# A plain first unit, swapped banks, tables in thirty pieces, and weight sums made by accumulating transfers

## The chip, the cores and the metric

The kernel runs on one core of a Trainium2 chip. The core has a matrix engine (TensorE, PE in the profile, with its weight loads as PEld), a vector engine (VectorE, DVE), a scalar engine (ScalarE, ACT), a general one (GpSimd, POOL) and an engine that issues transfers (SyncE, SP), each with its own instruction queue that runs in order. Sixteen DMA engines move data between the chip's memory (HBM) and the core's on-chip memory. The metric is the device time of one launch in microseconds (us), the median over runs. The profile is one further execution.

## The reference

A stack of two layers over 512 tokens of width 1024, in 32-bit floats. Each layer is a half-step feed-forward block, a mixing block and another half-step feed-forward block, each behind an RMS norm; a last norm ends it.

```python
def swiglu(h, w_gate, w_up, w_down):
    return (jax.nn.silu(h @ w_gate) * (h @ w_up)) @ w_down

for l in range(DEPTH):                                  # DEPTH = 2
    x = x + 0.5 * swiglu(rmsnorm(x, ffn1_norm[l]), ...)  # FFN1, D_FF = 2816
    h = rmsnorm(x, mix_norm[l])
    ...                                                  # pooling heads, dilated attention with rotary q, k
    x = x + mixed @ w_out[l]
    x = x + 0.5 * swiglu(rmsnorm(x, ffn2_norm[l]), ...)  # FFN2
return rmsnorm(x, final_norm)
```

## The kernel before

The activations are kept transposed: `x[c]` is a tile of 128 channels by 512 tokens, c from 0 to 7. Every product of 32-bit numbers is made of three matmuls: each operand is split into a high part, rounded by a copy on ScalarE (`whi`, L357; `ah`), and a rest, which VectorE subtracts (`wlo`, L360; `al`), and high by high, low by high and high by low are added up.

A feed-forward block walks over six *units* of the 2816 hidden columns (`UNITS`, L38): first a small unit of 256, then five big units of 512. The gate and up products of a unit are not done plainly: activations and weights are cut into two by two blocks (token halves and channel halves against channel halves and gate/up columns), and seven products of sums of blocks are formed instead of eight (`PORD`, L39, is their order; `norm.block` picks the activation side). The sums of activations (`s_n`, `sh_n`, `sl_n`) are made once a block by `norm.fold` (L421), the sums of weight quarters for each unit anew by VectorE: `total` (L251) adds three quarters in two steps (L254, L258) for product 6, `every` (L264) adds that sum to a fourth (L266) for product 4, `across` (L260) adds two (L262) for product 7. A big unit does this twice (`cp` 0 and 1), so eight such sums of 128x1024; a small unit has four. The seven results are put together in `evacuate` (L616) on their way out of the accumulator banks: `px_f` holds products 1, 6, 7 and 4, `pz_f` products 2, 5 and 3. There are two banks under each of the tags A and B, and units alternate which tag `px_f` gets (L609).

After a unit's products, its hidden activations are transposed (`pt_f`, L600) during the next unit, and its down products (`pd_f`, L382 to L384) are put between that unit's steps; their result is added to `x` (L708). A steady unit on PE is 168 matmuls of 512 columns for the gate and up products, 96 for the down products, and 16 transposes.

The weights come through a list of jobs in the order of their use. `take` (L367) hands out a job's split weights, splits the job that stands two further on (`AHEAD`), and then `pump` (L332) starts as many loads of 512 KB as the cap of eleven live tiles lets it, all on SP's queue. `later`, `lazy` and `slow` are lists of work for VectorE and ScalarE, emitted by `flush` (L198) one step on.

At a block's start `norm.square` (L472) and `finish_col` (L489) sum squares on PE (`ms_n`), and one small power on POOL (L498) gives the norm's factor. Results of the first unit wait for it before they can be scaled. In layer 0's FFN1 this runs in `startup` (L119), while `x` is still being loaded.

The rotary tables (cosine and sine of position times frequency) are made by a generator (`tables`, L149) whose pieces of five to seven VectorE operations are called at the end of steps 6 and later in units 1 and 2 of the very first FFN1 (L683).

Of the kernel before, what the change touches and what calls it, by code (L numbers as in the profile page):

```python
# [10 lines left out]
F32 = mybir.dt.float32  # L11
F32R = mybir.dt.float32r
# [4 lines left out]
P = 128  # L17
S = 512
# [60 lines left out]
def trunk(ctx: ExitStack, tc: tile.TileContext, a: dict):  # L79
# [39 lines left out]
    def startup(norm):  # L119
# [21 lines left out]
        for c in range(KD):  # L141
            norm.fold(c)
            if c < 2:
                divide(c)
            if c == 4:
                divide()
            flush()

    def tables():  # L149
# [26 lines left out]
        reduce(turn)  # L176
        yield
        add_times(turn, far, M2)
        add_times(turn, far, M3)
        reduce(turn)  # L180
        yield
        nc.vector.tensor_tensor(ang, ang, turn, op=ALU.add)
        reduce(ang)
# [6 lines left out]
        nc.vector.tensor_tensor(k, k, k, op=ALU.mult)  # L190
        nc.vector.tensor_scalar(cosT, k, -2.0, 1.0, op0=ALU.mult, op1=ALU.add)
# [12 lines left out]
    class Load:  # L204


        def __init__(self, src, n, temps=0):
            self.src, self.n, self.temps, self.tile = src, n, temps, None

    class Job:  # L210


        def __init__(self, key, n, needs, get, pre=None, done=None):
            self.key, self.n, self.needs, self.get, self.pre, self.done = key, n, needs, get, pre, done
            self.part = None
# [3 lines left out]
    state = {"live": 0, "temps": 0, "load": 0, "split": 0, "taken": 0, "cap": SLOTS}  # L219
# [9 lines left out]
    def product_jobs(i, l, u):  # L229
# [3 lines left out]
        made, out = {}, []  # L233
# [12 lines left out]
        first = next(iter(made.values()))  # L246
        first.temps = cps
        loads.extend(made.values())
        both = {}

        def total(cp):  # L251

            b11, b12, b22 = (made[q + (cp,)].tile for q in ((0, 0), (0, 1), (1, 1)))
            nc.vector.tensor_tensor(b11, b11, b12, op=ALU.add)  # L254
            both[cp] = t4([P, D], F32, f"sum_{i}{l}_{u}_{cp}")
            state["live"] += 1
            state["temps"] -= 1
            nc.vector.tensor_tensor(both[cp], b11, b22, op=ALU.add)  # L258

        def across(cp):  # L260
            b12, b22 = made[0, 1, cp].tile, made[1, 1, cp].tile
            nc.vector.tensor_tensor(b12, b12, b22, op=ALU.add)  # L262

        def every(cp):  # L264
            b21 = made[1, 0, cp].tile
            nc.vector.tensor_tensor(b21, b21, both[cp], op=ALU.add)  # L266
            free()

        for p in PORD:
            for cp in range(cps):  # L270
                q = {k: made[k + (cp,)] for k in quarters + [(0, 1), (1, 1)]}
# [822 lines left out]
```

## Time and profile before

| what | value |
|---|---|
| median of 3 runs | 1922.75 us (1921.74 to 1922.85) |
| the profiled execution's own time | 1919.58 us |
| its span, first to last instruction | 1917.8 us |
| mean granted clock of PE | 0.986 of full |
| PE busy | 1857.2 us, 97% |
| VectorE busy | 1444.4 us, 75% |
| ScalarE busy | 950.4 us, 50% |
| POOL busy | 116.9 us, 6% |

PE is the engine that is nearly always busy. The span is read by looking where it is not, and at which clock it runs. Busy shares of the other engines are means over stages with different limits, so each stage has to be looked at by itself.

### The profile page before, as it was taken

The page shows a single profiled execution, that of the slowest core. Times are in us where ns is not written, and L with a number is a line of the kernel's source. Part 1 is how long each engine was busy: PE and PEld are TensorE (multiplying, and loading weights), DVE is VectorE, ACT ScalarE, POOL GpSimd, SP SyncE. Part 2 cuts the span into 40 slices and gives each one's busy share as a digit, 9 for nine tenths or more (in the row PEclk, how much of TensorE's full clock was granted, in tenths as well). Part 3 has the DMA queues.
Part 4 walks back from the last instruction along what each step waited for, and adds up shares of the span by engine and source line. Part 5 has one row for each costly group of instructions (what it writes and reads, how often), then busy time and mean ns, then how long its engine had stood idle before and what let it go on. Part 6 is the DMA issues. An engine that isn't in the chain of part 4 may idle for free.

```text
span 1917.8 us, 23563 instructions
## 1 busy us (share of the span) xinstructions
PE 1857.2 (97%) x8966; PEld 1551.3 (81%) x8966; DVE 1444.4 (75%) x2041; ACT 950.4 (50%) x1474; POOL 116.9 (6%) x105
## 2 busy tenths in 40 slices
PE   6989999999999999999989999999999989999998
PEld 5868888898877888888878888888888778888887
DVE  6996677647887986778688777675688688777675
ACT  6444344436665553444464444444476565444444
POOL 0000000013230000000000000000323200000000
PEclk7999999999999999999999999999999999999999
DMA  5223333125451233422313322340454223232321
GB/s 183 88 79 100 128 110 107 64 76 145 113 158 56 66 121 99 132 96 97 105 50 116 121 88 88 99 148 17 126 134 126 89 94 116 99 99 96 102 77 45
DMA packets 59696, 194.36 MB, mean 101 GB/s; under 512 B 7920, under 2 KB 8064, under 8 KB 59584
## 3 DMA queue, kind: packets, MB, share of 16 engines
q1 hardware_dynamic: 59440, 192.57, 31.9%
q8 instruction: 70, 1.15, 0.2%
q0 software_dynamic: 144, 0.29, 0.1%
q14 instruction: 42, 0.34, 0.1%
HBM read 171.87 MB, written 2.10 MB: 91 GB/s over the span
## 4 chain that ended last, share of the span: by engine, by line
PE 86%; DVE 8%; ACT 2%; issue 2%; DMA 1%; POOL 1%; SPq 0%; DVEq 0%; POOLq 0%; ACTq 0%
PE pd_f L384 8%; PE pd_f L383 8%; PE pd_f L382 8%; PE px_f L658 8%; PE px_f L655 8%; PE px_f L657 8%; PE pz_f L655 6%; PE pz_f L658 6%; PE pz_f L657 6%; PE pv_m L747 3%; PE ps_m L814 2%; PE pt_m L827 2%; PE pt_f L600 2%; DVE wlo L360 1%; PE po_m L843 1%
## 5 line engine op out<-in xcount | busy, mean ns | idle before, releaser
L360 DVE TENSOR_TENSOR wlo<-raw,whi 128x1024 fp32r<-128x1024 f32 (+2 forms) x421 | 502.0, 1198 | 55.4 <-ACT whi L357 50.4
L357 ACT ACTIVATE whi<-raw 128x1024 fp32r<-128x1024 f32 (+2 forms) x421 | 421.7, 1026 | 220.3 <-DVE wlo L360 63.9
L384 PE MATMUL pd_f<-ah_f,wlo 128*128 128x512 f32 (+1 forms) x736 | 282.2, 383 | 3.1 <-DVE wlo L360 3.1
L382 PE MATMUL pd_f<-ah_f,whi 128*128 128x512 f32 (+1 forms) x736 | 281.5, 382 | 1.0 <-ACT ah_f L400 1.0
L383 PE MATMUL pd_f<-al_f,whi 128*128 128x512 f32 (+1 forms) x736 | 280.7, 381 | 1.0 <-DVE al_f L403 1.0
L708 DVE SCALAR_TENSOR_TENSOR x<-pd_f,x 128x512 f32<-128x512 f32 x184 | 127.0, 690 | 168.8 <-PE pd_f L384 165.5
L592 ACT ACTIVATE c_f<-c_f,rcol_n 128x256 f32<-128x256 f32 (+1 forms) x144 | 70.3, 492 | 272.4 <-DVE c_f L637 102.5
L384 PEld LDWEIGHTS pd_f<-ah_f,wlo 128*128 128x128 f32 x736 | 138.7, 188 | 33.5 <-DVE wlo L360 7.7
L383 PEld LDWEIGHTS pd_f<-al_f,whi 128*128 128x128 f32 x736 | 138.8, 189 | 28.8 <-DVE al_f L403 2.3
L655 PE MATMUL px_f<-whi,ah_n 128*128 128x512 f32 (+1 forms) x384 | 145.9, 380 | 15.7 <-DVE x L937 11.5
L382 PEld LDWEIGHTS pd_f<-ah_f,whi 128*128 128x128 f32 x736 | 138.9, 189 | 27.4 <-ACT ah_f L400 1.9
L655 PE MATMUL px_f<-whi,sh_n 128*128 128x512 f32 (+1 forms) x384 | 144.1, 375 | 5.7 <-ACT c_f L622 5.7
L658 PE MATMUL px_f<-wlo,ah_n 128*128 128x512 f32 (+1 forms) x384 | 145.2, 378 | 1.2 <-DVE wlo L360 1.2
L658 PE MATMUL px_f<-wlo,sh_n 128*128 128x512 f32 (+1 forms) x384 | 144.1, 375 | 1.9 <-DVE wlo L360 1.9
L658 PE MATMUL pz_f<-wlo,sh_n 128*128 128x512 f32 (+1 forms) x384 | 143.3, 373 | 2.1 <-DVE wlo L360 2.1
L657 PE MATMUL px_f<-whi,al_n 128*128 128x512 f32 (+1 forms) x384 | 145.3, 378 | 0.0
L655 PE MATMUL pz_f<-whi,sh_n 128*128 128x512 f32 (+1 forms) x384 | 143.7, 374 | 0.6 <-DVE c_f L624 0.3
L657 PE MATMUL px_f<-whi,sl_n 128*128 128x512 f32 (+1 forms) x384 | 143.7, 374 | 0.0
L657 PE MATMUL pz_f<-whi,sl_n 128*128 128x512 f32 (+1 forms) x384 | 143.1, 373 | 0.0
L819 ACT ACTIVATE e_m<-e_m,nmx_m 128x512 f32<-128x512 f32 x96 | 69.4, 723 | 78.7 <-DVE nmx_m L817 78.1
L655 PEld LDWEIGHTS px_f<-whi,ah_n 128*128 128x128 f32 x384 | 74.3, 193 | 30.1 <-DVE x L937 11.9
L817 DVE CUSTOM_DVE_ANT_0 e_m<-ps_m,gbias 128x512 f32<-128x512 f32 x96 | 65.9, 686 | 33.8 <-PE ps_m L814 33.3
(206 smaller groups left out, 3580.4 us busy)
## 6 DMA issues: line engine op xcount, KB each, us to landing
raw<-in_gu SPq DMA_DIRECT2D x160, 512.0 KB, 3.3
raw<-in_dn SPq DMA_DIRECT2D x80, 512.0 KB, 3.3
raw<-in_wqk SPq DMA_DIRECT2D x24, 512.0 KB, 5.4
qq_m<-hl_q_m SPq DMA_DIRECT2D x48, 256.0 KB, 4.2
raw<-in_wo SPq DMA_DIRECT2D x16, 512.0 KB, 5.3
raw<-in_gs SPq DMA_DIRECT2D x15, 512.0 KB, 4.9
raw<-in_wv SPq DMA_DIRECT2D x16, 384.0 KB, 3.1
kk_m<-hl_k_m SPq DMA_DIRECT2D x48, 128.0 KB, 2.3
```

Of the source, the lines that this page charges most:

```text
L357: nc.scalar.activation(hi[:, o:e], raw[:, o:e], AF.Copy)
L360: nc.vector.tensor_tensor(lo[:, o:e], raw[:, o:e], hi[:, o:e].bitcast(F32), op=ALU.subtract)
L382: nc.tensor.matmul(ps, hi[:, o:o + P], act[0], start=start, stop=False)
L383: nc.tensor.matmul(ps, hi[:, o:o + P], act[1], start=False, stop=False)
L384: nc.tensor.matmul(ps, lo[:, o:o + P], act[0], start=False, stop=stop)
L592: nc.scalar.activation(c[:, :w], src[:, :w], AF.Silu, scale=r)
L655: nc.tensor.matmul(ps, bh, hi[:, o], start=(k == 0 and p in (1, 2, 5)), stop=False, skip_group_check=True)
L657: nc.tensor.matmul(ps, bl, hi[:, o], start=False, stop=False, skip_group_check=True)
L658: nc.tensor.matmul(ps, bh, lo[:, o], start=False, stop=(k == 3), skip_group_check=True)
L708: nc.vector.scalar_tensor_tensor(x[d], ps, 0.5, x[d], op0=ALU.mult, op1=ALU.add)
L817: nc.vector.tensor_tensor_reduce(e, ps, gbias[:, o:o + S], -0.125, 3.0e38, ALU.add, ALU.min, nmx[hd][:, it:it + 1])
L819: nc.scalar.activation(e, e, AF.Exp, bias=nmx[hd][:, it:it + 1], scale=-1.0, accum_out=den[hd][:, it:it + 1])
```

## The change

Five things are changed together.

First, the small unit of FFN1 in both layers becomes a plain product (`plain_unit`). It takes its weights as four tiles of 128x1024 (`gc`, four splits in place of seven), with no sums of weights, and multiplies them by the four token blocks of 128 with all eight channel tiles, 96 matmuls of 512 columns in place of 168 of 256; four banks (two A, two B) hold the results until they are scaled. `fold` makes one more split for it (`a2`). FFN2's small unit stays as it was.

Second, `px_f` and `pz_f` swap bank tags, so that a block's first unit has `px_f` in B.

Third, the tables come in some thirty pieces of one or two VectorE operations, called from step 2 on in units 1, 2 and 3.

Fourth, the sums of weight quarters are no longer VectorE's. A quarter is loaded into a tile, and further quarters are added to it by transfers from POOL's queue that accumulate into their destination (`accum_op=ALU.add`). In a big unit there are 14 loads in place of 12 and 10 accumulating transfers of 512 KB, eight from HBM and two from another tile; `add_up` issues one per waiting tile at each `pump`, and `add` issues the others once the tile's earlier split is done.

Fifth, `startup` loads `x` and the weights in another order, splits two weight tiles in halves, and issues the squares between the folds.

```diff
-        for c in range(1, 4):
+        nc.sync.dma_start(x[1], a["xT"][1])
+        nc.sync.dma_start(x[2], a["xT"][2])
+        load(2)
+        nc.sync.dma_start(x[3], a["xT"][3])
+        for c in range(4, KD):
+            if c % 2 == 0:
+                load()
             nc.sync.dma_start(x[c], a["xT"][c])
-        load()
-        for c in range(4, KD):
-            nc.sync.dma_start(x[c], a["xT"][c])
+        nc.sync.dma_start(ident, a["ident"])
         pump()
-        nc.sync.dma_start(ident, a["ident"])
         pos = a["positions"]
         nc.gpsimd.dma_start(col, a["col"])
         nc.gpsimd.dma_start(pos_i, bass.AP(tensor=pos.tensor, offset=pos.offset, ap=[[0, P], [1, S]]))
...
             nc.tensor.matmul(warm, idle[:, 0:P], idle, start=True, stop=True)
         for c in range(KD):
             norm.fold(c)
-            if c < 2:
-                divide(c)
-            if c == 4:
-                divide()
+            if c < 4:
+                divide(c % 2)
             flush()
+            if c > 0:
+                norm.square(c - 1)
+        norm.square(KD - 1)
...
         def reduce(t):
             nearest(k, t, 1.0 / TWO_PI)
-            for c in (C1, C2, C3):
-                add_times(t, k, -c)
+            yield
+            add_times(t, k, -C1)
+            yield
+            add_times(t, k, -C2)
+            yield
+            add_times(t, k, -C3)
+            yield
 
 
         nc.vector.tensor_copy(ang, pos_i)
         nc.vector.tensor_scalar(ang, ang, col[:, 0:1], None, op0=ALU.mult)
+        yield
         nearest(far, ang, 2.0**-17)
+        yield
         add_times(ang, far, -2.0**17)
         yield
-        reduce(ang)
-        yield
+        yield from reduce(ang)
...
         def quarter(kh, n, cp):
-            ap = a[f"gs{i}"][l, kh, n] if small else a[f"gu{i}"][l, u, kh, n, cp]
-            made[kh, n, cp] = Load(ap, D)
-
-        quarters = [(0, 0), (1, 0)]
-        for kh, n in quarters:
-            for cp in range(cps):
-                quarter(kh, n, cp)
-        for cp in range(cps):
-            quarter(0, 1, cp)
-            quarter(1, 1, cp)
-        first = next(iter(made.values()))
-        first.temps = cps
-        loads.extend(made.values())
-        both = {}
-
-        def total(cp):
-
-            b11, b12, b22 = (made[q + (cp,)].tile for q in ((0, 0), (0, 1), (1, 1)))
-            nc.vector.tensor_tensor(b11, b11, b12, op=ALU.add)
-            both[cp] = t4([P, D], F32, f"sum_{i}{l}_{u}_{cp}")
-            state["live"] += 1
-            state["temps"] -= 1
-            nc.vector.tensor_tensor(both[cp], b11, b22, op=ALU.add)
-
-        def across(cp):
-            b12, b22 = made[0, 1, cp].tile, made[1, 1, cp].tile
-            nc.vector.tensor_tensor(b12, b12, b22, op=ALU.add)
+            return a[f"gs{i}"][l, kh, n] if small else a[f"gu{i}"][l, u, kh, n, cp]
+
+        def block(q, cp, adds=()):
+            ld = Load(quarter(*q, cp), D, [quarter(*q2, cp) for q2 in adds])
+            loads.append(ld)
+            return ld
+
+        def add(dst, src):
+            nc.gpsimd.dma_start(dst, src, accum_op=ALU.add)
 
         def every(cp):
-            b21 = made[1, 0, cp].tile
-            nc.vector.tensor_tensor(b21, b21, both[cp], op=ALU.add)
+            add(held[2, cp].tile, held[6, cp].tile)
             free()
 
         for p in PORD:
             for cp in range(cps):
-                q = {k: made[k + (cp,)] for k in quarters + [(0, 1), (1, 1)]}
                 key = ("g", i, l, u, p, cp)
-                tile_of = lambda k, q=q: (lambda: q[k].tile)
+                needs, done = [], free
                 if p == 1:
-                    job = Job(key, D, [q[0, 0]], tile_of((0, 0)))
+                    needs = [block((0, 0), cp)]
+                    done = lambda cp=cp: add(held[1, cp].tile, quarter(0, 1, cp))
                 elif p == 2:
-                    job = Job(key, D, [q[1, 0]], tile_of((1, 0)))
+                    needs, done = [block((1, 0), cp)], None
                 elif p == 6:
-                    job = Job(key, D, [q[0, 0], q[0, 1], q[1, 1]], lambda cp=cp: both[cp],
-                              pre=lambda cp=cp: total(cp), done=lambda cp=cp: every(cp))
-                elif p == 5:
-                    job = Job(key, D, [], tile_of((0, 0)), done=free)
+                    needs = [block((1, 1), cp, ((0, 0), (0, 1)))]
+                    done = lambda cp=cp: every(cp)
                 elif p == 7:
-                    job = Job(key, D, [], tile_of((0, 1)), pre=lambda cp=cp: across(cp), done=free)
+                    needs = [block((0, 1), cp, ((1, 1),))]
                 elif p == 3:
-                    job = Job(key, D, [], tile_of((1, 1)), done=free)
-                else:
-                    job = Job(key, D, [], tile_of((1, 0)), done=free)
-                out.append(job)
+                    needs = [block((1, 1), cp)]
+                if needs:
+                    held[p, cp] = needs[0]
+                ld = held[{5: 1, 4: 2}.get(p, p), cp]
+                out.append(Job(key, D, needs, lambda ld=ld: ld.tile, done=done))
...
         for n, u in enumerate(UNITS):
+            if i == 1 and u == NU:
+                for g in range(4):
+                    plain(("c", l, g), a["gc"][l, g], D)
+                continue
...
+    def add_up():
+        for ld in list(adding):
+            nc.gpsimd.dma_start(ld.tile, ld.adds.pop(0), accum_op=ALU.add)
+            if not ld.adds:
+                adding.remove(ld)
...
     def pump():
+        add_up()
         while state["load"] < len(loads):
             ld = loads[state["load"]]
-            if state["live"] + 1 + state["temps"] + ld.temps > state["cap"]:
+            if state["live"] + 1 > state["cap"]:
...
+                if self.n % 3 == 0:
+                    a2 = t2([P, 2, H], F32R, f"a2_{nm}")
+                    self.a2[k] = a2
+                    nc.scalar.activation(a2[:, 0, :], xs[:, 1, :], AF.Copy)
+                    later.append(lambda: nc.vector.tensor_tensor(a2[:, 1, :], xs[:, 1, :], a2[:, 0, :].bitcast(F32),
+                                                                 op=ALU.subtract))
...
+        def tile_of(self, t, c):
+
+            if t >= 2 and c < 4:
+                both = (self.a2[c][:, 0, :], self.a2[c][:, 1, :])
+            else:
+                z = 0 if c < 4 else 1 if t < 2 else 2
+                both = (self.ah[c % 4][:, z, :], self.al[c % 4][:, z, :])
+            return tuple(v[:, t % 2 * P:(t % 2 + 1) * P] for v in both)
...
-            xs = [bank("AB"[n % 2], f"px_{nm}_{u}_{i}") for i in range(2)]
+            xs = [bank("BA"[n % 2], f"px_{nm}_{u}_{i}") for i in range(2)]
...
-                    zs.update({i: bank("BA"[n % 2], f"pz{p}_{nm}_{u}_{i}") for i in range(2)})
+                    zs.update({i: bank("AB"[n % 2], f"pz{p}_{nm}_{u}_{i}") for i in range(2)})
...
-                    if first and n in (1, 2) and z >= 6:
+                    if first and n in (1, 2, 3) and z >= 2:
                         next(rotary, None)
...
+        def plain_unit(u):
+
+            ps = [bank("AABB"[t], f"pc_{nm}_{t}") for t in range(4)]
+
+            def part(t, k, w, o):
+                ah, al = norm.tile_of(t, k)
+                hi, lo = (v[:, o:o + S] for v in w)
+                nc.tensor.matmul(ps[t], ah, hi, start=(k == 0), stop=False)
+                nc.tensor.matmul(ps[t], al, hi, start=False, stop=False)
+                nc.tensor.matmul(ps[t], ah, lo, start=False, stop=(k == KD - 1))
+
+            for g in range(3):
+                flush()
+                w = take("c", l, g)
+                for z in range(2):
+                    for t in range(4):
+                        part(t, 2 * g + z, w, z * S)
+                    flush()
+            w = take("c", l, 3)
+            norm.finish_col()
+            cs = [t2([P, S], F32, f"cc_{nm}_{t}") for t in range(4)]
+            for t in range(4):
+                for z in range(2):
+                    part(t, 6 + z, w, z * S)
+                flush()
+                activation_block(cs[t], ps[t], t, S // 2)
+            for j in range(2):
+                turns.append(lambda j=j: turn(u, j, cs, j, S // 2))
...
-            products(n, u)
+            if n == 0 and which == 1:
+                plain_unit(u)
+            else:
+                products(n, u)
```

What this moves is seen in the order of instructions. VectorE, in unit 1 of layer 0's FFN1, before; `kmul`, `ang`, `turn` and `far` belong to the tables, `wlo` is a weight split, `x` the addition of a down product:

```order
L262 TENSOR_TENSOR raw_371<-raw_371,raw_407 128x1024
L360 TENSOR_TENSOR wlo_704<-raw_279,whi_703 128x1024
L708 SCALAR_TENSOR_TENSOR x_66<-pd_f_5_2_731,x_66 128x512
L360 TENSOR_TENSOR wlo_727<-raw_371,whi_726 128x1024
L708 SCALAR_TENSOR_TENSOR x_67<-pd_f_5_3_740,x_67 128x512
L155 TENSOR_SCALAR kmul<-ang 128x512
L156 TENSOR_SCALAR kmul<-kmul 128x512
L159 SCALAR_TENSOR_TENSOR ang<-kmul,ang 128x512 x3
L360 TENSOR_TENSOR wlo_754<-raw_615,whi_753 128x512
L175 TENSOR_SCALAR turn<-far 128x512
L155 TENSOR_SCALAR kmul<-turn 128x512
L156 TENSOR_SCALAR kmul<-kmul 128x512
```

The same place after the change:

```order
L365 TENSOR_TENSOR wlo_549<-raw_108,whi_548 128x1024
L750 SCALAR_TENSOR_TENSOR x_64<-pd_f_5_0_575,x_64 128x512
L365 TENSOR_TENSOR wlo_571<-raw_110,whi_570 128x1024
L750 SCALAR_TENSOR_TENSOR x_65<-pd_f_5_1_584,x_65 128x512
L159 TENSOR_SCALAR kmul<-ang 128x512
L160 TENSOR_SCALAR kmul<-kmul 128x512
L365 TENSOR_TENSOR wlo_595<-raw_505,whi_594 128x512
L163 SCALAR_TENSOR_TENSOR ang<-kmul,ang 128x512
L365 TENSOR_TENSOR wlo_616<-raw_120,whi_615 128x1024
L750 SCALAR_TENSOR_TENSOR x_66<-pd_f_5_2_642,x_66 128x512
L365 TENSOR_TENSOR wlo_638<-raw_276,whi_637 128x1024
L750 SCALAR_TENSOR_TENSOR x_67<-pd_f_5_3_651,x_67 128x512
```

Between two weight splits there stood up to five rows of the tables (one of them three operations), and the sums of L262; now one or two, and no sum.

VectorE at the end of the mixing block and the start of FFN2 in layer 0, before; `x_70` and `x_71` are residual additions that free banks of the output projection, `sl_n` and `al_n` belong to the fold, and `raw_5100` is the quarter that product 1 uses:

```order
L360 TENSOR_TENSOR wlo_5243<-raw_5100,whi_5242 128x1024
L937 TENSOR_TENSOR x_70<-po_m_6_5247,x_70 128x512
L480 TENSOR_TENSOR sq_n_0_5140<-sq_n_0_5140,sq_n_5_5240 128x512
L254 TENSOR_TENSOR raw_5100<-raw_5100,raw_5104 128x1024
L258 TENSOR_TENSOR sum_5_0_5297<-raw_5100,raw_5106 128x1024
L457 TENSOR_TENSOR sl_n_5_5239<-s_n_5_5237,sh_n_5_5238 128x512
L458 TENSOR_TENSOR sl_n_5_5239<-s_n_5_5236,sh_n_5_5238 128x512
L446 TENSOR_TENSOR al_n_2_5162<-xs_n_6_5284,ah_n_2_5161 128x512
```

After:

```order
L365 TENSOR_TENSOR wlo_5171<-raw_5020,whi_5170 128x1024
L982 TENSOR_TENSOR x_70<-po_m_6_5176,x_70 128x512
L497 TENSOR_TENSOR sq_n_0_5064<-sq_n_0_5064,sq_n_5_5168 128x512
L465 TENSOR_TENSOR sl_n_5_5167<-s_n_5_5165,sh_n_5_5166 128x512
L466 TENSOR_TENSOR sl_n_5_5167<-s_n_5_5164,sh_n_5_5166 128x512
L454 TENSOR_TENSOR al_n_2_5086<-xs_n_6_5214,ah_n_2_5085 128x512
```

The two sums, L254 and L258, are gone from between the squares (`sq_n`) and the fold; the rest of the sequence stands as it did.

POOL, from the first transfers to the power of the first norm (`npow`), before:

```order
L122 DMA vecs<-in_vecs 128x60
L136 DMA col<-in_col 128x2
L137 DMA pos_i<-in_positions 128x512
L498 ISA
L498 TENSOR_TENSOR rcol_n_357<-rcol_n_357,npow 128x4
```

After; `raw_116`, `raw_118`, `raw_120` and `raw_276` are tiles of the first big unit that are added to as soon as they are loaded (L322), `raw_108` and `raw_110` tiles that are added to once their first split is done (L258):

```order
L140 DMA pos_i<-in_positions 128x512
L322 DMA raw_116<-in_gu 128x1024
L322 DMA raw_118<-in_gu 128x1024
L322 DMA raw_120<-in_gu 128x1024
L322 DMA raw_116<-in_gu 128x1024
L322 DMA raw_118<-in_gu 128x1024
L322 DMA raw_276<-in_gu 128x1024
L258 DMA raw_108<-in_gu 128x1024
L258 DMA raw_110<-in_gu 128x1024
L515 ISA
L515 TENSOR_TENSOR rcol_n_383<-rcol_n_383,npow 128x4
```

Eight accumulating transfers now stand ahead of that power in POOL's queue.

## Rows read from the trace of the kernel before

**Rows 1.** page, part 1: PE busy us, share of the span, instructions

```profile
PE 1857.2 (97%) x8966; PEld 1551.3 (81%) x8966; DVE 1444.4 (75%) x2041; ACT 950.4 (50%) x1474; POOL 116.9 (6%) x105
```

**Rows 2.** windows: stretch, busy us of each engine, PEclk, DMA share, GB/s

```profile
54.00:105.00 51.00, 46.19 (x204) 37.00 (x204) 48.53 (x69) 20.53 (x30) 0.00 (x0) 0.98 0.31 98
...
1000.00:1051.00 51.00, 51.00 (x235) 42.41 (x235) 44.11 (x57) 25.88 (x38) 0.00 (x0) 1.00 0.34 109
1056.00:1118.00 62.00, 62.00 (x282) 51.33 (x282) 45.50 (x53) 27.08 (x36) 0.00 (x0) 1.00 0.31 102
```

**Rows 3.** timeline of PE at unit starts: start us, duration us, line, operation, count

```profile
55.02 0.40 PE L655 MATMUL px_f<-whi,ah_n 128*128 128x512 f32 x1
...
60.49 0.71 PE L600 MATMUL pt_f<-ident,c_f 128*128 128x128 f32 x5
...
120.24 0.60 PE L600 MATMUL pt_f<-ident,c_f 128*128 128x128 f32 x4
...
1001.13 0.40 PE L655 MATMUL px_f<-whi,ah_n 128*128 128x512 f32 x1
...
1006.60 0.60 PE L600 MATMUL pt_f<-ident,c_f 128*128 128x128 f32 x4
...
1056.50 0.71 PE L600 MATMUL pt_f<-ident,c_f 128*128 128x128 f32 x5
```

**Rows 4.** groups by form, VectorE: xcount | busy us, mean ns

```profile
L480 DVE TENSOR_TENSOR sq_n<-sq_n,sq_n 128x512 f32<-128x512 f32 x42 | 28.8, 685 | 0.6
...
L254 DVE TENSOR_TENSOR raw<-raw,raw 128x1024 f32<-128x1024 f32 x44 | 53.5, 1217 | 0.0
```

**Rows 5.** timeline of PE, startup, with idle time and releaser in brackets

```profile
33.02 0.58 PE L655 MATMUL px_f<-whi,sh_n 128*128 128x256 f32 x1 [5.14 <-ACT c_f L622]
...
44.85 0.39 PE L655 MATMUL pz_f<-whi,sh_n 128*128 128x256 f32 x1
```

**Rows 6.** timeline of VectorE, startup

```profile
14.03 0.69 DVE L446 TENSOR_TENSOR al_n<-xs_n,ah_n 128x512 fp32r<-128x512 f32 x1 [0.94 <-ACT ah_n L439]
...
30.05 0.68 DVE L458 TENSOR_TENSOR sl_n<-s_n,sh_n 128x512 fp32r<-128x512 f32 x1
```

**Rows 7.** timeline of ScalarE, startup

```profile
9.89 0.61 ACT L357 ACTIVATE whi<-raw 128x512 fp32r<-128x512 f32 x1
...
11.15 0.42 ACT L433 ACTIVATE ah_n<-xs_n 128x256 fp32r<-128x256 f32 x1
11.47 0.71 ACT L428 ACTIVATE xs_n<-x,vecs 128x512 f32<-128x512 f32 x1
...
12.61 0.72 ACT L428 ACTIVATE xs_n<-x,vecs 128x512 f32<-128x512 f32 x1
...
30.53 2.17 ACT L474 ACTIVATE sq_n<-x 128x512 f32<-128x512 f32 x4
```

**Rows 8.** timeline of PE, start of FFN1 in layer 1

```profile
968.84 0.28 PE L655 MATMUL px_f<-whi,ah_n 128*128 128x256 f32 x1
...
975.02 0.39 PE L658 MATMUL pz_f<-wlo,ah_n 128*128 128x256 f32 x1 [2.91 <-DVE wlo L360]
```

**Rows 9.** timeline of VectorE, start of FFN1 in layer 1

```profile
984.43 1.22 DVE L360 TENSOR_TENSOR wlo<-sum,whi 128x1024 fp32r<-128x1024 f32 x1
```

**Rows 10.** timeline of PE, start of FFN2 in layer 0

```profile
624.47 0.58 PE L655 MATMUL px_f<-whi,ah_n 128*128 128x256 f32 x1 [5.76 <-DVE x L937]
...
628.85 0.28 PE L658 MATMUL pz_f<-wlo,ah_n 128*128 128x256 f32 x1
...
631.79 0.39 PE L658 MATMUL px_f<-wlo,sh_n 128*128 128x256 f32 x1 [0.35 <-DVE wlo L360]
```

**Rows 11.** DMA queues, 1056 to 1118: packets, MB, share of 16 engines

```profile
q1 hardware_dynamic: 1728, 6.29, 31.1%
```

**Rows 12.** DMA queues, 0 to 10

```profile
q1 hardware_dynamic: 947, 1.90, 56.8%
q0 software_dynamic: 144, 0.29, 20.1%
```

More of the change, by code (lines that the diff above doesn't have):

```diff
@@ L190, in tables @@
         nc.vector.tensor_tensor(k, k, k, op=ALU.mult)
+        yield
         nc.vector.tensor_scalar(cosT, k, -2.0, 1.0, op0=ALU.mult, op1=ALU.add)
@@ L204, in trunk, with __init__ @@
     class Load:
-        def __init__(self, src, n, temps=0):
-            self.src, self.n, self.temps, self.tile = src, n, temps, None
+        def __init__(self, src, n, adds=()):
+            self.src, self.n, self.adds, self.tile = src, n, list(adds), None
     class Job:
-        def __init__(self, key, n, needs, get, pre=None, done=None):
-            self.key, self.n, self.needs, self.get, self.pre, self.done = key, n, needs, get, pre, done
+        def __init__(self, key, n, needs, get, done=None):
+            self.key, self.n, self.needs, self.get, self.done = key, n, needs, get, done
             self.part = None
@@ L218, in trunk @@
     AHEAD, SLOTS = 2, 11
-    state = {"live": 0, "temps": 0, "load": 0, "split": 0, "taken": 0, "cap": SLOTS}
+    adding = []
+    state = {"live": 0, "load": 0, "split": 0, "taken": 0, "cap": SLOTS}
     def free():
@@ L232, in product_jobs @@
         cps = 1 if small else 2
[L233 removed]
+        out, held = [], {}
         def quarter(kh, n, cp):
[L236 to L262 removed]
+            return a[f"gs{i}"][l, kh, n] if small else a[f"gu{i}"][l, u, kh, n, cp]
[5 more added lines that the diff above has]
+            nc.gpsimd.dma_start(dst, src, accum_op=ALU.add)
         def every(cp):
[L265 to L266 removed]
+            add(held[2, cp].tile, held[6, cp].tile)
             free()
@@ L326, in load @@
         state["live"] += 1
-        state["temps"] += ld.temps
+        if ld.adds:
+            adding.append(ld)
         for z in range(pieces):
@@ L342, in prepare_sums @@
                 load()
-        if job.pre is not None:
-            job.pre()
-            job.pre = None
+            while ld.adds:
+                add_up()
     def divide(half=None):
@@ L372, in take @@
             divide()
-        nxt = i + AHEAD + 1
-        if nxt < len(jobs) and jobs[nxt].pre is not None and all(ld.tile is not None for ld in jobs[nxt].needs):
-            prepare_sums(jobs[nxt])
         pump()
@@ L424, in fold @@
             if c == 0:
-                self.xs, self.ah, self.al, self.sh, self.sl = ([None] * 4 for _ in range(5))
+                self.xs, self.ah, self.al, self.sh, self.sl, self.a2 = ([None] * 4 for _ in range(6))
             k, nm = c % 4, f"{self.name}_{c}"
@@ L661, in step @@
                 if cp == cps - 1:
-                    if first and not n and p in (1, 2):
-                        for k in range(4 * p - 4, 4 * p):
-                            norm.square(k)
-                            flush()
                     if not n and p == 6:
@@ L1057 @@
         arrays[f"gu{i}"] = big.transpose(0, 6, 1, 7, 2, 4, 3, 5, 8).reshape(L, NU, 2, 2, 2, P, D)
-        small = pair[..., NB:].reshape(L, 2, 4, P, 2, 2, P)
-        arrays[f"gs{i}"] = small.transpose(0, 1, 5, 3, 2, 4, 6).reshape(L, 2, 2, P, D)
+        small = pair[..., NB:]
+        if i == 1:
+            arrays["gc"] = small.reshape(L, 4, 2, P, S).transpose(0, 1, 3, 2, 4).reshape(L, 4, P, D)
+        else:
+            arrays["gs2"] = small.reshape(L, 2, 4, P, 2, 2, P).transpose(0, 1, 5, 3, 2, 4, 6).reshape(L, 2, 2, P, D)
         dn = v[f"ffn{i}_w_down"]
```

8 lines of the change are left out of this document (5 added, 3 removed).

## The prediction

> **What bounds the kernel now.** I read the engine line of the page first: PE is busy 1857.2 of 1917.8 us [rows 1], so all that can be won without taking work from PE is the 60.6 us in which it does nothing, and what it loses at the lower of its two clock levels (1.2 instead of 2.4 GHz). The windows then show where that is. In a steady stretch, 1056 to 1118, PE works 62.00 of 62 us at a granted clock of 1.00, VectorE only 45.50, and the DMA engines are busy 0.31 of the time [rows 2]: PE sets the pace and VectorE has 16 us to spare. The first big unit of layer 0 is different: in 54:105 PE works 46.19 of 51 us and VectorE 48.53, where the same stretch of layer 1 (1000:1051) has PE at 51.00 and VectorE at 44.11 [rows 2]. So VectorE binds in one unit of twenty, and elsewhere only at the four starts of a feed-forward block, read below from PE's waits.
>
> **Tables in thirty pieces.** The first transposes of units 1 and 2 stand at 60.49 and 120.24 in layer 0, 59.75 us apart, and at 1006.60 and 1056.50 in layer 1, 49.90 apart [rows 3]: the same work, and the rotary tables are the only thing that layer 0 has more. They cost 9.85 us, because pieces of five to seven operations go into VectorE's queue between two weight splits and the split that PE waits for stands behind them. After the change a piece is one or two operations, at most about 0.7 us each (the adds of the same width take 685 ns [rows 4]), and only a dozen pieces come in unit 1. VectorE's load there is then the 44.11 of layer 1, less eight sums of 1.22 us (the row of L254 gives 1217 ns, and the other three lines the like [rows 4]), plus some 8 us of pieces: 42 of 51 us, so PE hides it. Units 2 and 3 take the rest, where VectorE has 16 us free already. I take all of it, 9.9; at least 7, if single pieces still stand before a late split.
>
> **Plain first unit, startup.** PE's matmuls go from 168 of 256 columns to 96 of 512. From 55.02 to 60.49 24 matmuls of 512 columns take 5.47 us, 0.228 each [rows 3], so the new work is 96 x 0.228 = 21.9 us, against 168 x 0.12 (the spacing in the stretch at full clock, half a 512) = 20.2: 1.7 more. But PE waits here. It idles 5.14 us up to 33.02, for a copy of ScalarE's that stands behind the first summed quarter, and runs at the low clock from there till 44.85 [rows 5]. After the change the plain product can't end before VectorE has folded all activations, and the fold begins later: ScalarE gets four more copies of 256 columns (0.42), two more weight halves (0.61) and three squares (2.17/4) ahead of the fourth fold, which starts at 12.61 now [rows 7]; 1.7 + 1.2 + 1.6, less 0.1 of overlap at each, is 3.9, so the operation at 14.03 [rows 6] moves to 17.9. From 14.03 to the end of the last fold (30.05 + 0.68) are 16.7 us [rows 6]; a split and two sums, 1.22 each at this width [rows 4], leave this stretch, 13.1 stay, and seven additions of squares, 0.6 each, come in: 17.9 + 13.1 + 4.2 = 35.2. The split of the third weight tile is next, done at 36.3. PE has done 48 matmuls by then (till about 23) and waits some 13 us. Of the 46 that are left it does about 12 at the low clock (0.456), then 34 at 0.228, with 1 us for the eight small sums: 5.5 + 7.8 + 1 = 14.3, and the first big unit starts at 50.6 instead of 55.02 [rows 3]. I take 4.5. If all 46 run at the low clock, as before for 11.8 us after its wait [rows 5], it is 58 and 3 us are lost; with no low clock 7 are won.
>
> **Plain first unit, layer 1.** Before, PE waits 2.91 us at 975.02 and twice more, at half clock between, for VectorE [rows 8]. The split at 984.43 is the first behind the last fold [rows 9]. Two sums (2.4 us) stand ahead of it and go, so the split of the third weight tile ends at 984.43 - 2.4 + 1.2 = 983.2; the new small subtractions come earlier, beside PE's down products. PE has till then 48 matmuls that need nothing late (968.8 [rows 8] + 10.9 = 979.7), waits 3.5 us, then has 46 x 0.228 + 1 = 11.5, and I add 2 for a low clock after the wait: 996.7 against 1001.13 [rows 3], 4.4 won (between 2 and 6.4).
>
> **FFN2's small units.** They stay products of seven. Now PE waits 5.76 us at 624.47 for the residual add that frees its bank, runs at the low clock to 628.85, and is released at 631.79 by the split of the summed quarter [rows 10]. With the banks swapped the first wait goes; the next one late is that same split, 2.4 us earlier, since the two sums ahead of it go. So 2.4 is the most; if PE comes out of the new wait at the low clock, 22 matmuls cost up to 2 of it again. I take 1.7, twice: 3.4 (0.8 to 4.8).
>
> **Sums by accumulating transfers.** Elsewhere the eight sums of a unit lie beside PE, so taking them from VectorE brings nothing there: 0. What they cost on the DMA side is the open point, since no accumulating transfer is in the trace. A big unit loads 14 tiles of 512 KB instead of 12, and adds 10 accumulates of 512 KB, all on POOL's one queue, issued in order. The queue of plain loads moved 6.29 MB in 62 us at 31.1% of the 16 engines, twelve loads, so one load is 19.3/12 = 1.61 us of all sixteen [rows 11]. The packets of POOL's queue, as far as there are any, took 20.1% of 10 us for 0.29 MB, those of SP's queue in the same stretch 56.8% for 1.90 MB [rows 12]: 7.0 us per MB against 3.0, or 3.6 us for a tile. So an accumulate is bounded by 1.61 (a load) and, by the dearest copy in the trace, 3.6; one that took twice that would cost 7.2. A unit then needs 14 x 1.61 = 22.5, plus 16 to 36 (or 72) us of the engines, 39 to 59 (or 95) of the unit's 61.8. Below 3.9 us each PE still sets the pace. I take 2.6, the middle of the two rows, 49 us of 61.8, hidden: an accumulate has most of a unit's time before its sum is split, and POOL has nothing else in a block but one small power at its start. That power waits behind accumulates, whose issue waits for a split that VectorE does just before it; 1 us at most.
>
> The Trainium skill speaks against this part. Its page "Collectives: The Full Stack" (section "The bandwidth ceiling: the fold count and why AG ≠ RS ≠ AR") says that an add inside the DMA engine needs two source reads, and so goes at half the rate of a copy. By it an accumulate is twice 1.61, 3.2 us, an estimate, and a unit 54 of 61.8 us: still hidden, with little left. No row here shows an accumulate.
>
> **Sum.** 9.9 + 4.5 + 4.4 + 3.4 = 22.2 from the profiled execution's 1919.58 us gives 1897.4. The median of the runs shown, 1922.75, lies 3.2 above that execution, so I say 1900.5.
>
> **The rivals.** First, the starts give nothing: the low clock lasts through the plain units, whose work is 1.7 us longer on PE, and the power comes late. Startup then loses 3, layer 1 gives 2 less 1, FFN2 0.8, the tables 7 to 9.9. That is 6 to 9 won, 1914 to 1917. For it: PE did stay low for 11.8 us after a wait of 5.14 [rows 5]; against: in FFN2 it was up again 4.4 us after 5.76 [rows 10]. Second, only the tables count, the starts giving half: 9.9 + 6 = 16, 1907; it lies inside the forecast's own range. Third, on the other side: the DMA engines become the bound. From 3.9 us per accumulate on, each us more costs 10 us in each of 20 big units. At three loads' worth, 4.83, a unit takes 22.5 + 48.3 = 71 instead of 61.8: 20 x 9 = 180 slower, less 22, about 2080; at 7.2 it takes 95, some 2560. It decides from 4.0 us. For it: POOL's packets are 2.3 times as dear as SP's [rows 12], ten of them stand in one queue, and reading the sum's old value comes on top. Against: those packets ran beside a full burst of loads, and the steady stretch leaves 69% of the engines free [rows 2]. That VectorE's relief has no effect at all is not a rival beside these, since I count it nowhere but at the starts.
>
> **Chances.** The forecast with its range (1893 to 1909) 0.67; the first rival 0.16; the DMA bound 0.17. A measurement of this kernel tells a change from none at about 0.2%, 3.8 us. Rival one lies mostly beyond it, at 0.13 faster and 0.03 the same; a DMA bound barely reached could also end level, 0.02. So faster 0.80, the same 0.05, slower 0.15. The range has to leave out no more than 0.2: from 1888, if every part gives its most (9.9 + 7 + 6.4 + 4.8 = 28, and 3 for what I do not see), to 1916.
>
> **What would show it.** Right: the transposes of units 1 and 2 in layer 0 about 50 us apart; the first unit's start near 50.6 and layer 1's 27.8 us after its last down product; one wait of about 3 us for the split in each FFN2 start; a steady unit still 62 us with PE at 62 and VectorE near 36, the DMA share at 0.6 to 0.9. Wrong: PE waiting in steady units for ScalarE's copies of summed tiles, with the DMA share near 1.00, or POOL's power late and PE held at the first big unit's bank.

## The result and the profile after

The changed kernel takes 1948.21 us (median of 4 runs, 1945.4 to 1953.8) against 1922.8 before. The ratio is 1.0134, with a 95% interval of 1.0106 to 1.0161: it is 1.3% slower, where 1900.5 us was forecast, and the time lies outside the range of 1888 to 1916.

The page of the changed kernel answers to [rows 1] with its engine line; below it stand POOL's and SP's DMA queues (packets, MB, share of 16 engines) and three kinds of transfer (count, KB, us from issue to landing):

```profile
PE 1866.0 (96%) x8822; PEld 1547.0 (80%) x8822; DVE 1239.0 (64%) x1848; ACT 954.3 (49%) x1457; POOL 301.3 (15%) x315
...
q1 hardware_dynamic: 65632, 214.60, 33.5%
q0 software_dynamic: 30384, 110.41, 30.6%
...
raw<-in_gu SPq DMA_DIRECT2D x200, 512.0 KB, 4.3
raw<-in_gu POOLq DMA_DIRECT2D x160, 512.0 KB, 9.3
raw<-in_dn SPq DMA_DIRECT2D x80, 512.0 KB, 5.6
raw<-raw POOLq DMA_DIRECT2D x42, 512.0 KB, 12.3
```

VectorE lost 205 us of work (1444.4 to 1239.0), but PE is busy 8.8 us longer with 144 matmuls fewer: more of its work ran at the low clock (mean granted 0.982 of full, 0.986 before), as the rows below show. The accumulates, 210 of 512 KB, took 30.6% of the 16 engines' 1944.2 us, 2.8 us of all sixteen each. From issue to landing they need 9.3 us from HBM and 12.3 from tile to tile, the load of a down weight 5.6 instead of 3.3.

Where the time went is read from the timeline of PE, at the places of [rows 3], with two waits among them. Two more rows of before come first, the first transposes of the third unit in layer 0's and layer 1's FFN1:

```profile
182.72 0.27 PE L600 MATMUL pt_f<-ident,c_f 128*128 128x128 f32 x1
...
1118.27 0.38 PE L600 MATMUL pt_f<-ident,c_f 128*128 128x128 f32 x2
```

After:

```profile
49.48 0.39 PE L672 MATMUL px_f<-whi,ah_n 128*128 128x512 f32 x1
...
54.93 0.27 PE L617 MATMUL pt_f<-ident,cc_f 128*128 128x128 f32 x1
...
104.81 0.38 PE L617 MATMUL pt_f<-ident,c_f 128*128 128x128 f32 x2
...
119.77 0.80 PE L675 MATMUL px_f<-wlo,sh_n 128*128 128x512 f32 x1 [4.36 <-DVE wlo L365]
120.36 0.63 PE L672 MATMUL px_f<-whi,sh_n 128*128 128x512 f32 x1
...
173.64 0.38 PE L617 MATMUL pt_f<-ident,c_f 128*128 128x128 f32 x2
...
1001.30 0.39 PE L672 MATMUL px_f<-whi,ah_n 128*128 128x512 f32 x1
...
1006.75 0.38 PE L617 MATMUL pt_f<-ident,cc_f 128*128 128x128 f32 x2
...
1056.60 0.27 PE L617 MATMUL pt_f<-ident,c_f 128*128 128x128 f32 x1
...
1073.17 0.80 PE L675 MATMUL px_f<-wlo,sh_n 128*128 128x512 f32 x1 [5.98 <-DVE wlo L365]
...
1126.49 0.38 PE L617 MATMUL pt_f<-ident,c_f 128*128 128x128 f32 x2
```

The first big unit starts at 49.48 instead of 55.02, and its first transposes come 5.6 us earlier. From there to those of the second unit it is 49.88 us instead of 59.75. Up to here the change has won 15.4 us. Then the second unit takes 68.83 instead of 62.48, and in layer 1's FFN1 69.89 (1056.60 to 1126.49) instead of 61.77. In the middle of these two units PE waits 4.36 and 5.98 us for a weight split of product 6, and comes out of the wait at the low clock: 0.80 and 0.63 us for a matmul that takes 0.39, and a granted clock of 0.50 from 119 to 123. Set side by side over all units, the first transposes of one to those of the next, the change wins 25.0 us at the places where it was meant to (startup 5.6, unit 1 9.9, layer 1's FFN1 6.3, the two FFN2 1.6 each, with the mixing block in front of them) and loses 51.4 in the other units: 31.1 in the four second units of a block (6.3, 7.3, 8.1, 9.4), 20.3 in the twelve later ones and the tail.

What PE waits for is one step back, on VectorE, and that waits for a transfer:

```profile
118.49 1.23 DVE L365 TENSOR_TENSOR wlo<-raw,whi 128x1024 fp32r<-128x1024 f32 x1 [7.49 <-DMA raw<-raw]
...
1071.90 1.22 DVE L365 TENSOR_TENSOR wlo<-raw,whi 128x1024 fp32r<-128x1024 f32 x1 [9.11 <-DMA raw<-raw]
```

This split reads product 6's second tile, which is there (ScalarE copied it at 110.05), and writes `wlo`. In the built program the on-chip tile that it writes into was, till then, product 6's first tile, and the accumulate from tile to tile (`raw<-raw`) still reads that. In POOL's timeline these are the second and third unit (L322: sums before the split, L258: after it):

```profile
98.35 2.65 POOL L322 DMA_DIRECT2D raw<-in_gu  x3 [9.18 <-DMA raw<-in_gu]
100.00 2.78 POOL L258 DMA_DIRECT2D raw<-in_gu  x2
102.54 1.13 POOL L258 DMA_DIRECT2D raw<-raw  x1
104.67 0.86 POOL L258 DMA_DIRECT2D raw<-raw  x1 [1.00 <-DVE wlo L365]
...
161.21 2.64 POOL L322 DMA_DIRECT2D raw<-in_gu  x3 [8.78 <-DMA raw<-in_gu]
165.68 0.86 POOL L258 DMA_DIRECT2D raw<-in_gu  x1 [1.82 <-DVE wlo L365]
168.06 0.86 POOL L258 DMA_DIRECT2D raw<-in_gu  x1 [1.52 <-DVE wlo L365]
171.38 0.86 POOL L258 DMA_DIRECT2D raw<-raw  x1 [2.45 <-DVE wlo L365]
173.51 0.86 POOL L258 DMA_DIRECT2D raw<-raw  x1 [1.26 <-DVE wlo L365]
```

At 98.35 POOL, which issues in order and had waited 9.18 us for an earlier sum to land, sends out seven accumulates within 7 us, the two from tile to tile last. The DMA engines from 98 to 122 (busy tenths in 40 slices, then POOL's queue, then the last two's time to land):

```profile
DMA  9619599998999999999999999999999999999999
...
q0 software_dynamic: 1008, 3.67, 79.6%
...
raw<-raw POOLq DMA_DIRECT2D x2, 512.0 KB, 16.7
```

They are full from 102 to 122; 3.67 MB, seven accumulates, fill 79.6% of 24 us, 2.7 each. The two tile-to-tile transfers land 16.7 us after their issue, in the median. In the third unit the same seven are issued over 12 us, and little is waited for. Whether that spacing alone makes the later units lose less was not tried by itself.

### The profile page after: what moved, and what is told of

It is laid out like the page before. It is cut to its first block, busy times and chain, and to the rows that moved or that the text cites. A ratio compares the mean times of both kernels' runs of the same rounds, so it can differ in the third digit from the quotient of the medians.

```text
span 1944.2 us, 23866 instructions
## 1 busy us (share of the span) xinstructions
PE 1866.0 (96%) x8822; PEld 1547.0 (80%) x8822; DVE 1239.0 (64%) x1848; ACT 954.3 (49%) x1457; POOL 301.3 (15%) x315
## 3 DMA queue, kind: packets, MB, share of 16 engines
q0 software_dynamic: 30384, 110.41, 30.6%
## 5 line engine op out<-in xcount | busy, mean ns | idle before, releaser
L365 DVE TENSOR_TENSOR wlo<-raw,whi 128x1024 fp32r<-128x1024 f32 (+2 forms) x460 | 550.2, 1199 | 253.3 <-ACT whi L362 151.5
L362 ACT ACTIVATE whi<-raw 128x1024 fp32r<-128x1024 f32 (+2 forms) x460 | 471.9, 1030 | 375.2 <-DVE wlo L365 160.8
L322 POOL DMA_DIRECT2D raw<-in_gu x120 | 107.3, 1078 | 881.3 <-DMA raw<-in_gu 829.4
L675 PE MATMUL pz_f<-wlo,sh_n 128*128 128x512 f32 (+1 forms) x352 | 133.6, 380 | 0.5 <-DVE wlo L365 0.5
L672 PE MATMUL pz_f<-whi,sh_n 128*128 128x512 f32 (+1 forms) x352 | 133.8, 380 | 0.0
L675 PE MATMUL px_f<-wlo,ah_n 128*128 128x512 f32 (+1 forms) x352 | 133.6, 380 | 0.0
L674 PE MATMUL px_f<-whi,al_n 128*128 128x512 f32 (+1 forms) x352 | 133.6, 379 | 0.0
L672 PE MATMUL px_f<-whi,ah_n 128*128 128x512 f32 (+1 forms) x352 | 133.6, 379 | 0.0
L674 PE MATMUL pz_f<-whi,sl_n 128*128 128x512 f32 (+1 forms) x352 | 133.5, 379 | 0.0
L675 PEld LDWEIGHTS px_f<-wlo,sh_n 128*128 128x128 f32 x352 | 69.7, 198 | 48.1 <-DVE wlo L365 35.2
## 6 DMA issues: line engine op xcount, KB each, us to landing
raw<-raw POOLq DMA_DIRECT2D x42, 512.0 KB, 12.3
```

The lines of the kernel that those rows point to most:

```text
L322: nc.gpsimd.dma_start(ld.tile, ld.adds.pop(0), accum_op=ALU.add)
L362: nc.scalar.activation(hi[:, o:e], raw[:, o:e], AF.Copy)
L365: nc.vector.tensor_tensor(lo[:, o:e], raw[:, o:e], hi[:, o:e].bitcast(F32), op=ALU.subtract)
L672: nc.tensor.matmul(ps, bh, hi[:, o], start=(k == 0 and p in (1, 2, 5)), stop=False, skip_group_check=True)
L674: nc.tensor.matmul(ps, bl, hi[:, o], start=False, stop=False, skip_group_check=True)
L675: nc.tensor.matmul(ps, bh, lo[:, o], start=False, stop=(k == 3), skip_group_check=True)
```

## The experiments

What held the split was the first question. (The expectations say 2.95 us for an accumulate, which leaves out eight of the 210; it is 2.8.)

**Product 4's sum back on VectorE** (the two tile-to-tile transfers of a unit go, eight accumulates stay):

```diff
-            add(held[2, cp].tile, held[6, cp].tile)
+            nc.vector.tensor_tensor(held[2, cp].tile, held[2, cp].tile, held[6, cp].tile, op=ALU.add)
```

> Only the addition of product 6's sum to product 2's quarter goes back to VectorE (two of the ten accumulates of a big unit); the other eight stay. Theory 'slot': the split of product 6's second half waits for a tile that the transfer from tile to tile still reads, so PE's waits in the second big unit of each block (4.4, 4.3, 6.0 and 6.7 us, 6.4 to 9.4 with the low clock behind them) go, and most of the 1 to 3 us of the other units: 1903 to 1918 us. Theory 'load': the DMA engines are too full (0.78 busy in a steady unit), eight accumulates of ten remain, the waits stay at half or more: 1932 to 1946.

1892.05 us, ratio to before 0.9847 (0.9832 to 0.9861). Every full unit takes 61.64 to 61.67 us and PE waits in none. The same stretches as in [rows 2]:

```profile
54.00:105.00 51.00, 51.00 (x232) 42.27 (x231) 42.53 (x61) 25.44 (x36) 7.13 (x8) 1.00 0.66 180
105.00:167.00 62.00, 62.00 (x285) 51.54 (x284) 45.62 (x60) 28.11 (x37) 7.00 (x8) 1.00 0.78 201
1056.00:1118.00 62.00, 62.00 (x283) 51.48 (x283) 38.64 (x46) 27.86 (x36) 7.02 (x8) 1.00 0.70 189
```

PE is busy throughout although the DMA engines stay at 0.66 to 0.78. By its expectation "load" is out, though two accumulates in ten are gone here as well. 56 us hang on 42 of 210 accumulates.

**Product 4's accumulate from memory**: as many accumulates, as many bytes, but product 6's tile is free after its split.

```diff
-            add(held[2, cp].tile, held[6, cp].tile)
+            add(held[2, cp].tile, quarter(0, 0, cp))
```

> Product 4's accumulate reads a quarter from HBM in place of product 6's tile, so the number of accumulates and their bytes stay and product 6's tile is free after its split; product 4 gets another sum, and the output is another one. Theory 'slot': 1890 to 1900 us, with ten accumulates on the queue. Theory 'load': 1930 to 1950. A third, that a transfer from tile to tile is itself the dear one (12.3 us to land against 9.3): 1890 to 1900 and POOL's queue clearly below 30% of the 16 engines.

1894.57 us, ratio 0.9856 (0.9842 to 0.9871); every full unit takes 61.64 to 61.67 here too. Its page shows the queues as full and the landings as late as in the changed kernel, and the last line, from 105 to 105.3, the two accumulates that stand in place of those at 102.54 and 104.67:

```profile
q0 software_dynamic: 30384, 110.41, 31.3%
...
raw<-in_gu POOLq DMA_DIRECT2D x200, 512.0 KB, 9.6
raw<-in_dn SPq DMA_DIRECT2D x80, 512.0 KB, 6.7
...
raw<-in_gu POOLq DMA_DIRECT2D x2, 512.0 KB, 19.9
```

These two land after 19.9 us, later than the 16.7 from tile to tile, and nothing waits for them. So in the units of this kernel neither the load on the engines nor the lateness of the sums costs anything; the tile that is held does. That theory is "slot", and this run shows it.

**Two ways to leave one more tile free.** A cap of 10 live weight tiles, and 26 large tiles against 24 small:

```diff
-    AHEAD, SLOTS = 2, 11
+    AHEAD, SLOTS = 2, 10
```

> All accumulates stay; the cap on live tiles is 10 in place of 11, so one more of the 25 tiles is free when a split needs one. Theory 'slot': the split no longer has to take the tile that the transfer has just read, the long waits shrink: 1912 to 1930 us. Theory 'load': one load less ahead makes nothing better: 1945 to 1960.

```diff
-    NW, NT, WARM = 25, 26, 10
+    NW, NT, WARM = 26, 24, 10
```

> The changed kernel with all its accumulates; only the on-chip tiles are shared out differently: 26 of 4 KB and 24 of 2 KB in place of 25 and 26. In the order of waits the second split of product 6 then no longer waits for the transfer from tile to tile; the first that does is product 4's own split, some 40 us later in a unit. Theory 'slot' (the transfer is late, but only the tile that it holds makes PE wait): the long waits go, units return to 61.7, 1890 to 1900 us. Theory 'load' (the DMA engines are too full with ten accumulates): the waits move to other splits, 1930 to 1950.

Both times missed what "slot" gave: 1972.91 us, 1.0270 (1.0255 to 1.0286), outside both ranges, and 1936.25 us, 1.0073 (1.0055 to 1.0092), inside the range of "load". By its time alone the second run would have spoken for "load"; the run with ten accumulates from memory and the waits here speak against that. In both, PE's long waits are still four, in the second unit of each block, and stand one split later, at the down weights. For the 26 tiles:

```profile
121.72 0.79 PE L384 MATMUL pd_f<-ah_f,whi 128*128 128x512 f32 x1 [5.02 <-ACT whi L362]
...
713.07 0.80 PE L384 MATMUL pd_f<-ah_f,whi 128*128 128x512 f32 x1 [8.81 <-ACT whi L362]
```

The waits in the built programs say why: the copy `whi` of the next split, that of the down weights, now takes product 6's first tile, and waits for the same transfer. With the cap of 10 the timeline of ScalarE shows it in the same unit:

```profile
125.48 1.06 ACT L362 ACTIVATE whi<-raw 128x1024 fp32r<-128x1024 f32 x1 [14.29 <-DMA raw<-raw]
```

For the 26 tiles the profile names no releaser of the long waits of this copy; there the first tile-to-tile transfer is issued at 102.0, lands 18.5 us later, and the copy starts at 120.61. A free tile more moves the wait on by one allocation and no further; I had read from the order that it would move by half a unit. With the cap of 10, ScalarE's copies wait for loads of down weights too (69.9 us in ten waits), and PE's waits for the copies sum to 49.1 us.

**Plain copies in place of the accumulates** (the same in `add_up`; the sums are left out):

```diff
-            nc.gpsimd.dma_start(dst, src, accum_op=ALU.add)
+            nc.gpsimd.dma_start(dst, src)
```

> Every accumulating transfer is a plain copy of the same bytes on the same queue of POOL, so the sums are left out and the output is another one. If the add itself is dear (it reads its destination too), POOL's queue takes about half of its 2.95 us of the 16 engines for each transfer, the landing falls from 9.3 and 12.3 us to 6 or less, and the time to 1900 to 1920. If the queue itself is dear, share, landings and time stay within a tenth: 1940 to 1950.

1897.39 us (2 runs), ratio 0.9876 (0.9857 to 0.9896):

```profile
q0 software_dynamic: 30384, 110.41, 16.3%
...
raw<-in_gu POOLq DMA_DIRECT2D x160, 512.0 KB, 5.2
...
raw<-raw POOLq DMA_DIRECT2D x42, 512.0 KB, 2.9
```

The same packets and bytes on the same queue take 16.3% of 1895.5 us, 1.5 us each instead of 2.8, and land in 5.2 and 2.9 us. So the queue is not dear, the add is: 1.9 times a copy. These copies hold product 6's tile as well, but for 2.9 us, and every full unit takes 61.64 to 61.67.

**Product 4's accumulate alone**, all other sums on VectorE (the edit is against the kernel with all sums on VectorE, below):

```diff
-            nc.vector.tensor_tensor(b21, b21, both[cp], op=ALU.add)
+            nc.gpsimd.dma_start(b21, both[cp], accum_op=ALU.add)
```

> The opposite of the first experiment: all sums on VectorE but product 4's, which is an accumulate from tile to tile (two in a big unit, alone on POOL's queue). Theory 'queue' (it lands late because five or six accumulates at 2.95 us of all engines each stand before it): alone it lands in about 5 us, and little is waited for: 1898 to 1908 us, against 1902 with all sums on VectorE. Theory 'tile to tile is slow in itself': it lands in 10 us or more and PE waits as before, 1920 to 1950.

1900.64 us, ratio 0.9882 (0.9868 to 0.9897); the transfer lands in 4.9 us and every full unit takes 61.64 to 61.67. From tile to tile is not slow in itself; with this run and the one with ten accumulates from memory, what makes it late is what stands ahead of it in the queue.

**All sums on VectorE, the rest of the change kept; and the accumulates alone on the kernel before.** The code of the sums is that of the kernel before in the one, of the changed one in the other (`product_jobs`, `load`, `pump`, `take`).

> All sums of weight quarters back on VectorE as before the change; plain first unit, swapped banks, tables in pieces and startup stay. If the accumulates alone made it slower, the stretches won in the changed kernel stay won (5.6 at startup, 9.9 in unit 1, 6.3 at layer 1's FFN1, 1.6 at each FFN2): about 1923 - 25 = 1898 us, 1893 to 1903. If the plain units or the pieces also cost something in the big units, or need the relief of VectorE to be hidden: 1905 or more.

> The kernel before with nothing changed but the sums, which are accumulates. If the parts add up: 1922 and the 51 us that the big units lost in the changed kernel, less some 4 that the sums free at the block starts, about 1965 us (1955 to 1975). If the losses come from the plain unit's or the tables' order together with the accumulates: below 1945.

1901.85 us, ratio 0.9902 (0.9886 to 0.9919), and 1974.07 us, ratio 1.0272 (1.0254 to 1.0289). By the medians the accumulates cost 51 us put into the kernel before, and 46 on top of the other parts. The two are not the same loss. Of the 51, 9.5 lie at startup (first transposes at 70.02 instead of 60.49), where the small unit still needs sums, and ScalarE and PE wait for one that is late (PE 18.37 us, 5.14 before [rows 5]):

```profile
42.65 1.06 ACT L345 ACTIVATE whi<-raw 128x1024 fp32r<-128x1024 f32 x1 [15.67 <-DMA raw<-in_gs]
...
46.11 0.58 PE L640 MATMUL px_f<-whi,sh_n 128*128 128x256 f32 x1 [18.37 <-ACT c_f L607]
```

So a late sum does cost where nothing lies beside it; the plain first unit keeps the changed kernel from that.

The first experiment beats the kernel with all sums on VectorE by 10 us (6.8 between the two traces). With VectorE making all the sums, units 1 to 3 of layer 0 take 50.9, 63.0 and 62.4 us (49.9, 61.7 and 61.6 there), so the table pieces are then not wholly hidden. That is 3.0 us; another 3.6 lie between FFN1's last unit and FFN2's first transposes, and what makes them was not tried. To hide the tables it is enough that product 4's sums leave VectorE: with six of eight sums on it, the run with product 4's accumulate alone, units 1 to 3 take 49.88, 61.67 and 61.64.

**The tables alone**, on the kernel before (`tables` and its call as in the change):

```diff
-                    if first and n in (1, 2) and z >= 6:
+                    if first and n in (1, 2, 3) and z >= 2:
```

> The kernel before with nothing changed but the tables, which come in some thirty pieces over units 1, 2 and 3. Where VectorE still makes the sums the pieces are not wholly hidden: 59.8 us between the first transposes of units 1 and 2 become 50 to 51, units 2 and 3 keep 0.5 to 1.5 over 61.8, so 1912 to 1916 us. If VectorE hides all of it: 1910 to 1912.

1914.44 us, ratio 0.9954 (0.9937 to 0.9970). Unit 1 takes 50.83, and units 2 and 3 keep 62.97 and 62.37, as in the kernel with all sums on VectorE.

**The banks as before**, in the first experiment's kernel:

```diff
-            xs = [bank("BA"[n % 2], f"px_{nm}_{u}_{i}") for i in range(2)]
+            xs = [bank("AB"[n % 2], f"px_{nm}_{u}_{i}") for i in range(2)]
...
-                    zs.update({i: bank("AB"[n % 2], f"pz{p}_{nm}_{u}_{i}") for i in range(2)})
+                    zs.update({i: bank("BA"[n % 2], f"pz{p}_{nm}_{u}_{i}") for i in range(2)})
...
-            ps = [bank("AABB"[t], f"pc_{nm}_{t}") for t in range(4)]
+            ps = [bank("BBAA"[t], f"pc_{nm}_{t}") for t in range(4)]
```

> The first experiment's kernel with the bank tags as before the change (the products' px_f in A in a block's first unit, and the plain unit's four banks turned likewise). If the swap is worth what the wait for the residual add suggests, each FFN2 start waits again some 3 to 5 us for its bank and 1 to 2 us of it reach the end: 1894 to 1897 us against 1892. If the split that comes next would have been late anyway: 1891 to 1893.

1891.75 us, ratio 0.9830 (0.9816 to 0.9845), the same as with the swap. The wait for the bank comes back, as the timeline of PE shows, and costs nothing. I take it that what follows is late anyway; that was not tried by itself:

```profile
603.87 0.39 PE L672 MATMUL px_f<-whi,ah_n 128*128 128x256 f32 x1 [3.37 <-DVE x L982]
...
610.27 0.39 PE L672 MATMUL px_f<-whi,sh_n 128*128 128x256 f32 x1 [1.83 <-ACT c_f L639]
```

The version that beats both kernels is the first experiment's: product 4's sum on VectorE, 1892.05 us.

## Why the prediction was wrong

The step that failed is "hidden: an accumulate has most of a unit's time before its sum is split", priced at 0. It cost 56 us, by the first experiment. Its premise held: an accumulate costs 2.8 us of the 16 engines, where 2.6 was taken, below the 3.9 from which the prediction lets the engines bind, and in the changed kernel's units no sum was late for its own split (the run with ten accumulates from memory). I asked only who reads the sum. A transfer from tile to tile has a second user of time, its source: the tile stays taken till the transfer has landed. Before, VectorE read it and it was free 1.2 us later. And the very next weight split needed that tile. What cost was the time to landing, not the mean load: seven accumulates of 2.7 us each go out at once, the tile-to-tile ones last, and land after some 17 us.

The third rival had the right place (accumulates) and sign and the wrong mechanism: it decides from 4.0 us per accumulate by full engines, and 2.8 was measured. Its sign "PE waiting in steady units for ScalarE's copies of summed tiles" was nearly what came; it waited for VectorE's rest of a tile that was complete. I gave this side 0.17.

The page of the Trainium skill that was weighed, "Collectives: The Full Stack" ("The bandwidth ceiling: the fold count and why AG ≠ RS ≠ AR"), gave an add half the rate of a copy, told there of a reduce-scatter against an all-gather; 3.2 us by the prediction's estimate. The trace agrees with the ratio: 2.8 us against 1.5 for a copy on the same queue, 1.9 times.

The other terms came out near their sizes, not all by the way that was worked out. Startup: 5.6 for 4.5. Here VectorE's last fold and the third weight tile's split came as worked out, as the timeline of VectorE shows beside [rows 6] (35.2 was said for the fold's end):

```profile
33.81 1.41 DVE L497 TENSOR_TENSOR sq_n<-sq_n,sq_n 128x512 f32<-128x512 f32 x2
35.14 3.67 DVE L365 TENSOR_TENSOR wlo<-raw,whi 128x1024 fp32r<-128x1024 f32 x3
```

Tables: 9.9 for 9.9, though not by the pieces alone: with all sums on VectorE they leave 0.9 us in unit 1 and 1.8 in units 2 and 3. Layer 1's plain unit: 6.3 for 4.4, since PE came out of its waits at the full clock (granted 1.00 from 987 to 1001), not the low one for which I had added 2. FFN2: 1.6 for 1.7 each, near by luck. From the end of the output projection to the first transposes it takes 35.4 us before in both layers, 34.6 and 33.8 after; the other 0.8 of layer 0 lies in the mixing block, which is as it was. The one wait of some 3 us that was to show there did not come, but in layer 0 four of 0.41 to 1.09. And the swap of banks, which was to take the first wait away, is worth nothing: with it and all sums on VectorE it is 35.4 again. Summed, 25.0 against 22.2: had the failed step held, the time would have come near 1898 (1922.8 less 25.0), and ten accumulates that hold no tile do give 1894.57. The lower end of the range, 1888, was counted from the profiled execution, 3.2 below the base of the forecast; nothing hangs on it. Taking the sums from VectorE was said to bring nothing in steady units. It brings 0.1 us in each (61.65 for 61.77), already with product 4's alone.

## What to carry to other kernels

When work moves from an engine to a transfer, ask of every operand, sources too, when it is free again: it is held from issue to landing (here some 17 us), and the landing counts everything queued ahead. Enough bandwidth per unit of work says nothing on that. Where tiles are recycled one after the other, as here, one spare tile moves such a wait by one allocation; take the transfer away that holds the tile (here two sums out of ten back on an engine that had time), and keep the rest.

## What the runs showed of the hardware

An accumulating transfer of 512 KB took 2.8 us of the 16 DMA engines (2.9 alone on its queue: 9.5% of 62 us for two), the plain copy 1.5 on the same queue of POOL, and a load on SP's queue 1.61 [rows 11]; the 3.6 that the packets of [rows 12] gave for POOL's queue is not its price for a 512 KB tile. Alone, a tile-to-tile accumulate landed in 4.9 us; behind others, in steady units, in 10 to 18. PE's clock stood at its low level (1.2 GHz, granted 0.50 from 119 to 123) after the wait of 4.36 us in the midst of steady work, and at the full one (1.00 from 987 to 1001) through the waits of 1.41 and 1.28 us in layer 1's plain unit.
